# Fixed preparation steps beside each matrix product in an fp32 encoder layer

## The chip, the cores and the metric

One core of a Trainium2 chip runs the whole layer. The metric is the device time of one execution in microseconds (us); lower is better. The engines are PE (TensorE, the matrix products), ACT (ScalarE), DVE (VectorE), POOL (GpSimd) and SP (SyncE, which issues most DMAs). Each runs its own queue in order.

## The reference

For 512 tokens of width 1024, in fp32:

```
h = h + 1/2 * SwiGLU_1(RMSNorm(h))             # d_ff 2816: gate, up, down
u = RMSNorm(h) @ W_in
h = h + concat([MLA(u), DiffAttention(u)]) @ W_out
h = h + 1/2 * SwiGLU_2(RMSNorm(h))
h = h + sigmoid(RMSNorm(h) @ W_g + b_g) * RMSNorm(p @ W_p)
SwiGLU(u) = (silu(u @ w_gate) * (u @ w_up)) @ w_down
```

## The kernel before

**Precision.** A product of two fp32 matrices is three PE passes: each operand is split into a high part (a cast to fp32r, on ACT) and a low part (source minus high part, a DVE subtraction, `sub` at L97), and `mm3` adds high*high, high*low and low*high (L373 to L375). So every weight that streams in from HBM has to be cast and subtracted before PE can use it.

**The ffns.** Each takes its 22 blocks of 128 hidden columns in four groups (`FGROUPS`): one "plain" group of 4 and three of 6. A group computes gate and up for its blocks, and then the 8 row blocks of its down projection into `h`. The plain group multiplies straight away and meanwhile builds, from the normed activations, the operands that the other groups use (`Forms.build`: DVE, ACT and a little POOL work). The groups of 6 work in pairs of blocks: `pair` calls `seven` twice, once for gate and once for up. `seven` does a 2x2 block product in 7 block products instead of 8. Each product is 12 matmuls of 128x256 (4 contraction blocks x 3 passes). Three PSUM banks take them: `r2` products 1, 4 and 7, `r1` products 2 and 5, `r3` products 3 and 6. Between two products that share a bank, DVE or ACT must read what the first left there (L530, L531, L534, L537, L542, L545), and PE waits for that reading.

**Preparing weights.** `items` is the list of weight pieces in the order of use. A `Chunk` is one piece: load, cast, low part. A `Unit` serves one `seven`: it loads `ra`, `rb`, `rc` through SP; in `sums` POOL issues two DMAs that add further weights onto `rb` and `rc` in SBUF; then come casts and low parts for `xa`, `xb`, `xc`, two POOL additions in `ra` (L170, L171), and last cast and low part of `xs`, the halves of which are the left operands of products 1 (`S2`) and 6 (`S4`). Finished pieces lie in two pools of three tiles (`held` counts them); a unit takes three tiles, so a unit is prepared in one pool while the unit before it is used from the other.

**The written order.** In the ffns ACT, DVE and POOL run in the order in which the program is written. `advance()` writes the next step of the next item, or nothing if its pool is full, and subtracts the step's cost from `st["time"]`. `slot(us)` adds an allowance to `st["time"]`, capped at 1.5, and writes steps while it is positive. `nxt()` takes the next finished item, and writes its missing steps first if it is not finished; they are subtracted too. Between the ffns only PE's order is written by hand, and `chunk()`, which is `nxt(2)`, prepares some 26 chunks without any allowance.

**Around it.** `Norm` sums squares of `h` (square on ACT, addition on POOL at L319) and `col_rsqrt` multiplies that sum by ones on PE. `prep()` loads the latents' up-weights (`upraw`), `embed()` loads and splits `pT` and multiplies it, in turns of the attention loop that `FILL_STEPS` sets. `pe_norm()`, stepped beside the second ffn's down projections, reads its product back and sums squares. At the start, `first` holds the first gate and up chunks, loaded and split in halves.

Of the kernel before, what the change touches and what calls it, by code (L numbers as in the profile page):

```python
# [8 lines left out]
F32 = mybir.dt.float32  # L9
# [5 lines left out]
P = 128  # L15
S = 512
# [19 lines left out]

FILL_PRE = "TTTTTTTTTTTTTKTKTKTTT"
FILL_MID = "TKK"
FILL_STEPS = ("T", "TT", "TT", "TT", "T", "") + ("E", "") * 8
HEADS = "DDMDMDMMMMMM"  # L40

GC = {"ffn1": 0, "mix": 8, "ffn2": 16, "ple_in": 24, "ple_out": 32, "b_ple": 40,
# [7 lines left out]
def encoder_layer(ctx, tc, xT, pT, wst, gcols, rows, consts, out):  # L50
# [84 lines left out]
    class Unit:  # L135
        LO, HI = slice(0, S), slice(S, BLK)

        def __init__(self, which):
            self.which = which
            self.loads = [self.load_b, self.load_a]  # L140
            self.steps = [(0.0, self.sums, 0), (0.0, self.cast_a, 1), (1.2, self.cast_b, 1), (1.2, self.low_b, 0),
                          (0.0, self.cast_c, 0), (0.7, self.low_c, 0), (0.0, self.cast_s, 1), (1.2, self.low_s, 0)]

        def load_b(self):
            self.s0, self.s1 = take(BLK), take(BLK)
# [16 lines left out]
        def cast_b(self):  # L162
            self.xb = hl_tile(self.which, "xb")
            nc.scalar.copy(self.xb[:, 0, :], self.rb)
            sub(self.xa[:, 1, :], self.ra, self.xa[:, 0, :])

        def low_b(self):
# [10 lines left out]
        def low_c(self):  # L178
            sub(self.xc[:, 1, :], self.rc, self.xc[:, 0, :])

        def cast_s(self):
            self.xs = hl_tile(self.which, "xs")
            nc.scalar.copy(self.xs[:, 0, :], self.ra)  # L183

        def low_s(self):
            sub(self.xs[:, 1, :], self.ra, self.xs[:, 0, :])
            st["raws"] -= 1
            xa, xb, xc, xs = self.xa, self.xb, self.xc, self.xs

            self.out = [(xa, 0), (xa, S), (xb, 0), (xb, S), (xc, 0), (xs, 0), (xs, S)]  # L190
# [6 lines left out]
    def ffn_items():  # L197
        for f0, n, plain in FGROUPS:
            if plain:
                items.extend(Chunk(BLK) for _ in range(2 * n))  # L200
            else:
                items.extend(Unit(u % 2) for u in range(n))
            items.extend(Chunk(n * P, 0 if m < KT // 2 else 1) for m in range(KT))

    ffn_items()
    items.extend(Chunk(2 * 416) for _ in range(4))
# [29 lines left out]
        load_ahead()  # L236
        return True

    def slot(us, ahead=3):

        st["time"] = min(st["time"] + us, 1.5)
        load_ahead()
        while st["time"] > 0 and len(ready) < ahead and advance():
            pass

    def nxt(ahead=0):
        if used:
# [133 lines left out]
            mm3(ps, w[:, 0, c], w[:, 1, c], acts[k][:, 0, :], acts[k][:, 1, :], k == 0, k == n - 1)  # L381


    n1 = Norm("ffn1")
    pe_dram = drp.tile([KT, P, S], F32, name="pe_dram")
    rpe = const.tile([P, TT], F32, name="rpe")
    first = []
# [8 lines left out]
        nc.scalar.copy(it.hl[:, 0, a:b], it.raw[:, a:b])  # L396
        sub(it.hl[:, 1, a:b], it.raw[:, a:b], it.hl[:, 0, a:b])

    half = [(0, S), (S, BLK)]
    nc.scalar.dma_start(out=first[0].raw[:, :S], in_=first[0].src[:, :S])  # L400
    nc.scalar.activation(warm, warm, AF.Silu)
    nc.sync.dma_start(out=h[0], in_=xT[0])
    nc.sync.dma_start(out=first[1].raw[:, :S], in_=first[1].src[:, :S])
    for t in range(1, 4):
        nc.sync.dma_start(out=h[t], in_=xT[t])
    for it in first:
        nc.sync.dma_start(out=it.raw[:, S:], in_=it.src[:, S:])
    for t in range(4, KT):
        nc.sync.dma_start(out=h[t], in_=xT[t])
    st["raws"] = 2  # L410
    load_ahead()
    piece(first[0], 0, S)
    n1.add(0, False)
    piece(first[1], 0, S)
    for t in range(1, 4):
        n1.add(t, False)
    for it in first:
        piece(it, S, BLK)
    st["raws"] = 0
    for t in range(4, KT):  # L420
        n1.add(t, False)
    load_ahead()
    nc.sync.dma_start(out=cst, in_=consts)
    nc.sync.dma_start(out=row, in_=rows.partition_broadcast(P))
# [7 lines left out]
    for t in range(KT):  # L432
        n1.square(t)
        if t == 3:
            slot(3.0)
    held[0] -= 2

    def pe_norm():
        pe_acc = t2("pe_acc")
        for m in range(KT):  # L440
            pe = t2("pel")
            nc.gpsimd.dma_start(out=pe, in_=pe_dram[m])
            square_sum(pe_acc, pe, m == 0)
            yield
        r4 = col_rsqrt(pe_acc, DM)
        nc.vector.tensor_copy(out=rpe, in_=r4)
        yield
# [5 lines left out]
    class Forms:  # L453
# [10 lines left out]
        def build(self, kp):  # L464
            def v(t):
                return t.rearrange("p (a b) -> p a b", b=HS)

            def put(i, src):
                pg_ = page(f"fm{i}")
                d = pg_.rearrange("p x (a b) -> p x a b", b=HS)  # L470
                split(d[:, 0], d[:, 1], src)
                self.pg[kp][i] = pg_

            y = hl_tile(1, "y", F32)
            ks = (2 * kp, 2 * kp + 1, 2 * kp + 4, 2 * kp + 5)
            for i, k in enumerate(ks):
                nc.vector.scalar_tensor_tensor(out=y[:, i // 2, (i % 2) * S:(i % 2 + 1) * S], in0=h[k],
                                               scalar=g(self.name, k), in1=self.rbc, op0=ALU.mult, op1=ALU.mult)
                yield
            q = [y[:, i].rearrange("p (a b) -> p a b", b=S) for i in range(2)]  # L480
            b11, b12 = q[0][:, :, :HS], q[0][:, :, HS:]
            b21, b22 = q[1][:, :, :HS], q[1][:, :, HS:]
            n1, t2_, n3, n4 = [v(t2(f"f{i}")) for i in range(4)]
            nc.gpsimd.tensor_sub(n1, b11, b12)
            nc.gpsimd.tensor_sub(n3, b12, b22)
            for i, k in enumerate(ks):
# [11 lines left out]
            put(self.N4, n4)  # L498
            yield

        def at(self, i, k):
# [8 lines left out]
    MUL = 12 * 0.12  # L510

    def seven(forms, after=None):

        F_ = Forms
        A11, A12, S1, A22, S3, S2, S4 = nxt()
        r1, r2, r3 = psum("r1"), psum("r2"), psum("r3")
        q1, q2, q3 = t2("q1"), t2("q2"), t2("q3")
        lo, hi = slice(0, HS), slice(HS, S)

        def mul(r, left, i, start):  # L520
            x, c0 = left
            for k in range(4):
                c = slice(c0 + k * P, c0 + (k + 1) * P)
                bh, bl = forms.at(i, k)
                mm3(r[:, lo], x[:, 0, c], x[:, 1, c], bh, bl, start and k == 0, k == 3, skip_group_check=True)

        mul(r2, S2, F_.T2, True)
        slot(MUL)
        mul(r1, A11, F_.B11, True)
        nc.scalar.copy(q1[:, lo], r1[:, lo])  # L530
        nc.vector.tensor_sub(q1[:, hi], q1[:, lo], r2[:, lo])  # L531
        slot(MUL - 0.42)
        mul(r3, S1, F_.N1, True)
        nc.vector.tensor_add(q2[:, lo], r3[:, lo], q1[:, lo])  # L534
        slot(MUL - 0.42)
        mul(r2, S3, F_.N3, False)
        nc.vector.tensor_sub(q3[:, hi], r2[:, lo], q2[:, lo])  # L537
        slot(MUL - 0.42)
        mul(r1, A12, F_.B21, False)
        after(0, r1[:, lo])  # L540
        mul(r3, S4, F_.B22, False)
        nc.vector.tensor_add(q2[:, hi], r3[:, lo], q1[:, hi])  # L542
        after(1, q2[:, hi])
        mul(r2, A22, F_.N4, False)
        nc.vector.tensor_sub(q3[:, lo], r2[:, lo], q1[:, lo])  # L545
        after(2, q3)

    def ffn(norm, after, side=None, early=None):
        st_ = {}
# [16 lines left out]
        def pair(hts):  # L566
# [3 lines left out]
            def gate(i, c):  # L570
                if i < 2:
                    nc.scalar.activation(a0[:, i * HS:(i + 1) * HS], c, AF.Silu)
                    slot(MUL - 0.42 * i)
                else:
                    nc.scalar.activation(c, c, AF.Silu)
                    box["a1"] = c
                    slot(MUL - 0.42)

            def up(i, c):
                if i < 2:  # L580
                    nc.vector.tensor_mul(a0[:, i * HS:(i + 1) * HS], c, a0[:, i * HS:(i + 1) * HS])
                    slot(MUL - 0.42 * (i + 1))
                else:
                    nc.vector.tensor_mul(c, c, box["a1"])
                    put_ht(a0, hts)
                    put_ht(c, hts)
                    slot(MUL - 2.5)

            seven(forms, gate)
            seven(forms, up)  # L590
# [8 lines left out]
        for gi, (f0, n, plain) in enumerate(FGROUPS):  # L599
# [30 lines left out]
            for m in range(KT):  # L630
# [4 lines left out]
                last = gi == len(FGROUPS) - 1  # L635
                if last:
                    after(m)
                elif side is not None and gi > 0:
                    next(side, None)
                slot(0.68 * n - (1.5 if last else 0.75))  # L640
                build(2)

# [112 lines left out]
    def prep():  # L755

        up, off = [], 0
        for i, n in enumerate(UP):
            raw = raw_tile("upraw")
            nc.sync.dma_start(out=raw[:, :n], in_=wst[off:off + P * n].rearrange("(p c) -> p c", p=P))  # L760
            off += P * n
            uh, ul = page(f"uph{i}", (P, BLK), pool=scope["pgx"]), page(f"upl{i}", (P, BLK))
# [138 lines left out]
    def embed():  # L901
        pa = []
        for k in range(2):
# [2 lines left out]
            ah, al = t2("pTh", F32R), t2("pTl", F32R)  # L906
            split(ah, al, pt_)
            pa.append((ah, al))
        for m in range(KT):
            if m % 4 == 0:  # L910
                w = chunk()
# [415 lines left out]
```

## Time and profile before

| | |
|---|---|
| median of 3 runs | 1193.39 us (1191.41 to 1195.14) |
| the profiled execution | 1193.64 us |
| its span in the profile | 1191.9 us |
| PE busy | 1055.9 us, 89% of the span |
| DVE busy | 737.9 us, 62% |
| ACT busy | 505.4 us, 42% |
| POOL busy | 348.7 us, 29% |
| mean granted PE clock | 0.959 |

The span runs from the first to the last instruction; 1.7 us of the time lie outside it. PE's busy time counts overlapping matmuls and half-clock matmuls as busy, so the share says little about what stands between PE and its full speed: the waits do, stage by stage. The first ffn runs from 0 to about 410 us, projections and attention to about 692, the second ffn to about 1140, and the gate of the embedding to the end.

### The profile page before, as it was taken

Reading aid. Unit: us, or ns where it says so; the run is one execution under the profiler, and the core shown is the slowest. Engines: PE = TensorE matmul, PEld = TensorE weight load, DVE = VectorE, ACT = ScalarE, POOL = GpSimd, SP = SyncE. Lnnn points to the kernel's source line nnn. Section 1 sums busy time; section 2 is a strip of 40 time slices with the busy share of each in tenths; the row PEclk is TensorE's granted clock in tenths of the full one; section 3 lists DMA queues with packets and bytes.
Section 4 is the critical chain, followed back from the end, with each engine's and each line's share of the span. In section 5 each row is a group of like instructions: output and inputs, shape, how many; then the busy total and the mean of one; then the engine's idle time right before and its main releaser. Section 6 shows DMA issues by size and latency. Waiting matters only on the chain.

```text
span 1191.9 us, 15846 instructions
## 1 busy us (share of the span) xinstructions
PE 1055.9 (89%) x6076; PEld 912.4 (77%) x6076; DVE 737.9 (62%) x1230; ACT 505.4 (42%) x824; POOL 348.7 (29%) x305
## 2 busy tenths in 40 slices
PE   8987898889889999979999995777897789888998
PEld 6867887888888887856678873557885788788887
DVE  5686755663665658886888626455653574466574
ACT  6343422342333546575786423223432342234341
POOL 4224402430431300054543121014324440243130
PEclk9999999999999998989999997788999899999999
DMA  6156535644562542221120210145535653564251
GB/s 240 27 148 154 127 117 135 155 115 138 148 145 79 164 131 87 75 85 53 54 72 18 89 53 27 45 123 144 136 104 165 157 123 113 139 150 107 97 195 53
DMA packets 50667, 133.73 MB, mean 112 GB/s; under 512 B 5952, under 2 KB 6336, under 8 KB 50592
## 3 DMA queue, kind: packets, MB, share of 16 engines
q1 hardware_dynamic: 36720, 104.78, 26.9%
q0 software_dynamic: 12432, 25.57, 11.9%
q10 hardware_dynamic: 1440, 2.39, 0.5%
q8 instruction: 47, 0.77, 0.3%
q14 instruction: 28, 0.23, 0.1%
HBM read 126.02 MB, written 6.29 MB: 111 GB/s over the span
## 4 chain that ended last, share of the span: by engine, by line
PE 52%; DVE 13%; POOL 11%; ACT 10%; DMA 7%; issue 7%; SPq 0%; ACTq 0%; POOLq 0%; DVEq 0%
POOL ra L170 5%; PE ps_d L375 5%; PE ps_d L374 5%; PE ps_d L373 5%; PE r L373 4%; POOL ra L171 4%; PE r L375 3%; PE r L374 3%; DVE xa L97 3%; ACT xa L160 3%; ACT xs L183 2%; DMA ra<-in_wst_dram 2%; PE ps_in L373 2%; PE ps_in L374 2%; PE ps_in L375 2%
## 5 line engine op out<-in xcount | busy, mean ns | idle before, releaser
L124 ACT CAST hl<-raw 128x768 fp32r<-128x768 f32 (+3 forms) x112 | 97.4, 887 | 131.1 <-PE ps_d L375 43.4
L97 DVE TENSOR_TENSOR hl<-raw,hl 128x768 fp32r<-128x768 f32 (+3 forms) x116 | 129.8, 1131 | 36.9 <-ACT hl L124 34.4
L375 PE MATMUL ps_d<-ht,hl 128*128 128x512 f32 x352 | 141.0, 401 | 10.8 <-DVE hl L97 10.8
L373 PE MATMUL ps_d<-ht,hl 128*128 128x512 f32 x352 | 141.0, 400 | 7.0 <-ACT hl L124 3.8
L374 PE MATMUL ps_d<-ht,hl 128*128 128x512 f32 x352 | 140.8, 400 | 0.2 <-DVE ht L94 0.2
L170 POOL TENSOR_TENSOR ra<-ra,rb 128x512 f32<-128x512 f32 x36 | 72.7, 2019 | 231.6 <-DVE xa L97 228.6
L373 PE MATMUL r<-fm,xb 128*128 128x256 f32 x288 | 84.3, 293 | 16.9 <-DVE q L537 16.9
L375 PEld LDWEIGHTS ps_d<-ht,hl 128*128 128x128 f32 x352 | 68.2, 194 | 28.9 <-DVE hl L97 14.7
L183 ACT CAST xs<-ra 128x1024 fp32r<-128x1024 f32 x36 | 37.7, 1047 | 115.5 <-POOL ra L171 115.5
L373 PEld LDWEIGHTS ps_d<-ht,hl 128*128 128x128 f32 x352 | 67.9, 193 | 21.6 <-ACT hl L124 4.2
L97 DVE TENSOR_TENSOR xs<-ra,xs 128x1024 fp32r<-128x1024 f32 x36 | 44.3, 1230 | 63.0 <-ACT xs L183 63.0
L373 PE MATMUL r<-sa,xa 128*128 128x256 f32 x288 | 82.5, 287 | 0.0
L374 PE MATMUL r<-sa,xa 128*128 128x256 f32 x288 | 82.3, 286 | 0.0
L375 PE MATMUL r<-sa,xa 128*128 128x256 f32 x288 | 82.1, 285 | 0.0
L374 PE MATMUL r<-fm,xb 128*128 128x256 f32 x288 | 81.4, 283 | 0.0
L375 PE MATMUL r<-fm,xb 128*128 128x256 f32 x288 | 81.3, 282 | 0.0
L374 PEld LDWEIGHTS ps_d<-ht,hl 128*128 128x128 f32 x352 | 68.3, 194 | 14.8 <-DVE ht L94 0.5
L319 POOL TENSOR_TENSOR acc<-acc,sq 128x512 f32<-128x512 f32 x28 | 39.2, 1401 | 131.8 <-ACT sq L318 131.5
L97 DVE TENSOR_TENSOR xa<-ra,xa 128x1024 fp32r<-128x1024 f32 x36 | 44.1, 1224 | 47.4 <-ACT xa L160 47.4
L373 PE MATMUL r<-fm,xc 128*128 128x256 f32 x144 | 44.7, 311 | 31.9 <-DVE q L531 31.9
L373 PEld LDWEIGHTS r<-fm,xb 128*128 128x128 f32 x288 | 54.9, 191 | 22.6 <-DVE q L537 22.6
L155 POOL DMA_DIRECT2D rb<-in_wst_dram x36 | 31.9, 886 | 100.7 <-DMA rb<-in_wst_dram 50.0
(333 smaller groups left out, 3091.3 us busy)
## 6 DMA issues: line engine op xcount, KB each, us to landing
raw<-in_wst_dram SPq DMA_DIRECT2D x44, 512.0 KB, 3.4
rb<-in_wst_dram SPq DMA_DIRECT2D x36, 512.0 KB, 5.2
ra<-in_wst_dram SPq DMA_DIRECT2D x36, 512.0 KB, 3.6
raw<-in_wst_dram SPq DMA_DIRECT2D x48, 384.0 KB, 3.6
rc<-in_wst_dram SPq DMA_DIRECT2D x36, 256.0 KB, 5.2
rb<-in_wst_dram POOLq DMA_DIRECT2D x36, 256.0 KB, 4.3
rc<-in_wst_dram POOLq DMA_DIRECT2D x36, 256.0 KB, 6.9
raw<-in_wst_dram SPq DMA_DIRECT2D x19, 256.0 KB, 2.6
```

The lines of the kernel that those rows point to most:

```text
L97: nc.vector.tensor_sub(dst_l, src, dst_h.bitcast(F32))
L124: nc.scalar.copy(self.hl[:, 0, :self.n], self.raw[:, :self.n])
L155: nc.gpsimd.dma_start(out=self.rb[:, self.LO], in_=self.s1[:, self.HI], accum_op=ALU.add)
L160: nc.scalar.copy(self.xa[:, 0, :], self.ra)
L170: nc.gpsimd.tensor_add(ra[:, LO], ra[:, LO], self.rb[:, LO])
L171: nc.gpsimd.tensor_add(ra[:, HI], ra[:, HI], ra[:, LO])
L183: nc.scalar.copy(self.xs[:, 0, :], self.ra)
L319: (eng or nc.gpsimd).tensor_add(acc, acc, sq)
L373: MM(ps, lhsT=wh, rhs=ah, start=start, stop=False, **kw)
L374: MM(ps, lhsT=wh, rhs=al, start=False, stop=False, **kw)
L375: MM(ps, lhsT=wl, rhs=ah, start=False, stop=stop, **kw)
```

## The change

- **Units.** Eight steps become eleven: the low part of `xa` is a step of its own, and cast and low part of `xs` are done in two halves, the half for product 1 first. Units use the pools in the opposite turn, and the plain group's down chunks all use pool 0.
- **Fixed steps.** In `seven`, `steps(n)` writes 1, 2, 2, 1, 1, 2, 2 steps behind products 1 to 7 (11 in all). The slots in `gate` and `up` go.
- **Slots elsewhere.** `slot(us)` sets the allowance afresh, without a cap or a limit on finished items.
- **First bank.** ACT copies `r2` behind product 1 into `q2[:, hi]`; the DVE subtraction that read `r2` there now reads that copy, and stands behind product 4.
- **Start.** The first two chunks come in pieces of 256, 256 and 512 columns instead of two halves, in another order of DMAs; the first norm's additions are on DVE; one load less is counted ahead.
- **Side work.** `pe_norm` loads through SP, two ahead, and takes two steps behind each down block of the second group instead of one in the second and third; `upraw` has pages of its own; `embed` loads and splits `pT` in a turn of its own, five attention steps earlier; the pool tile of `Forms.build` is counted.

```diff
-FILL_STEPS = ("T", "TT", "TT", "TT", "T", "") + ("E", "") * 8
+FILL_STEPS = ("T", "TTE", "TT", "TT", "T", "") + ("E", "") * 8
...
-            self.steps = [(0.0, self.sums, 0), (0.0, self.cast_a, 1), (1.2, self.cast_b, 1), (1.2, self.low_b, 0),
-                          (0.0, self.cast_c, 0), (0.7, self.low_c, 0), (0.0, self.cast_s, 1), (1.2, self.low_s, 0)]
+            self.steps = [(0.0, self.sums, 0), (0.1, self.cast_a, 1), (0.1, self.cast_b, 1), (1.2, self.low_a, 0),
+                          (1.2, self.low_b, 0), (0.1, self.cast_c, 0), (0.7, self.low_c, 0),
+                          (0.1, self.cast_s0, 1), (0.7, self.low_s0, 0), (0.1, self.cast_s1, 0),
+                          (0.7, self.low_s1, 0)]
...
+        def low_a(self):
             sub(self.xa[:, 1, :], self.ra, self.xa[:, 0, :])
...
-        def cast_s(self):
+        def cast_s0(self):
             self.xs = hl_tile(self.which, "xs")
-            nc.scalar.copy(self.xs[:, 0, :], self.ra)
+            nc.scalar.copy(self.xs[:, 0, self.LO], self.ra[:, self.LO])
+
+        def low_s0(self):
+            sub(self.xs[:, 1, self.LO], self.ra[:, self.LO], self.xs[:, 0, self.LO])
...
-                items.extend(Unit(u % 2) for u in range(n))
-            items.extend(Chunk(n * P, 0 if m < KT // 2 else 1) for m in range(KT))
+                items.extend(Unit(1 - u % 2) for u in range(n))
+            items.extend(Chunk(n * P, 1 if m < KT // 2 and not plain else 0) for m in range(KT))
...
-    def slot(us, ahead=3):
+    def slot(us):
 
-        st["time"] = min(st["time"] + us, 1.5)
+        st["time"] = us
         load_ahead()
-        while st["time"] > 0 and len(ready) < ahead and advance():
+        while st["time"] > 0 and advance():
             pass
+
+    def steps(n):
+        load_ahead()
+        for _ in range(n):
+            advance()
...
-    n1 = Norm("ffn1")
+    n1 = Norm("ffn1", nc.vector)
...
+    for it in first:
+        load_piece(it, 0, 256, nc.scalar)
     nc.scalar.activation(warm, warm, AF.Silu)
+    for a, b in ((256, 512), (512, BLK)):
+        t0 = a // 128 - 2
+        for t in (t0, t0 + 1):
+            nc.sync.dma_start(out=h[t], in_=xT[t])
+        for it in first:
+            load_piece(it, a, b)
...
-        for m in range(KT):
-            pe = t2("pel")
-            nc.gpsimd.dma_start(out=pe, in_=pe_dram[m])
-            square_sum(pe_acc, pe, m == 0)
+        pes = []
+        for m in range(KT + 2):
+            if m < KT:
+                pes.append(t2("pel"))
+                nc.sync.dma_start(out=pes[m], in_=pe_dram[m])
+            if m >= 2:
+                square_sum(pe_acc, pes[m - 2], m == 2)
...
         mul(r2, S2, F_.T2, True)
-        slot(MUL)
+        nc.scalar.copy(q2[:, hi], r2[:, lo])
+        steps(1)
         mul(r1, A11, F_.B11, True)
         nc.scalar.copy(q1[:, lo], r1[:, lo])
-        nc.vector.tensor_sub(q1[:, hi], q1[:, lo], r2[:, lo])
-        slot(MUL - 0.42)
+        steps(2)
         mul(r3, S1, F_.N1, True)
         nc.vector.tensor_add(q2[:, lo], r3[:, lo], q1[:, lo])
-        slot(MUL - 0.42)
+        steps(2)
         mul(r2, S3, F_.N3, False)
         nc.vector.tensor_sub(q3[:, hi], r2[:, lo], q2[:, lo])
-        slot(MUL - 0.42)
+        nc.vector.tensor_sub(q1[:, hi], q1[:, lo], q2[:, hi])
+        steps(1)
         mul(r1, A12, F_.B21, False)
         after(0, r1[:, lo])
+        steps(1)
         mul(r3, S4, F_.B22, False)
         nc.vector.tensor_add(q2[:, hi], r3[:, lo], q1[:, hi])
         after(1, q2[:, hi])
+        steps(2)
         mul(r2, A22, F_.N4, False)
         nc.vector.tensor_sub(q3[:, lo], r2[:, lo], q1[:, lo])
         after(2, q3)
+        steps(2)
...
-                elif side is not None and gi > 0:
-                    next(side, None)
+                elif side is not None and gi == 1:
+                    for _ in range(2):
+                        next(side, None)
...
-            raw = raw_tile("upraw")
+            raw = page("upraw", (P, BLK), F32)
...
             pa.append((ah, al))
+        yield
         for m in range(KT):
```

## Rows read from the trace of the kernel before

**Rows 1.** Waits of PE: who waited for whom, us in total, times, longest.
```profile
PE r L373 <- DVE q L531: 31.9, 30, 2.8
PE r L373 <- ACT xs L183: 19.3, 3, 11.6
PE r L373 <- DVE q L537: 16.9, 28, 0.6
PE ps_g L373 <- ACT hl L124: 13.1, 2, 8.4
...
PE r L375 <- DVE xs L97: 9.1, 6, 1.8
PE ps_pe L373 <- ACT pTh L93: 7.5, 1, 7.5
...
PE ps_q L373 <- ACT latT L732: 3.3, 1, 3.3
...
PE ps_g L373 <- ACT act_ffn L361: 2.2, 1, 2.2
PE ps_ss L329 <- POOL acc L319: 2.1, 1, 2.1
```
**Rows 2.** PE in order of time: start, duration, idle time before it.
```profile
1051.16 0.28 PE L373 MATMUL r<-sa,xa 128*128 128x256 f32 x1
...
1053.92 0.28 PE L375 MATMUL r<-fm,xb 128*128 128x256 f32 x1
1054.73 0.39 PE L373 MATMUL r<-fm,xc 128*128 128x256 f32 x1 [0.53 <-DVE q L531]
```
**Rows 3.** DVE in order of time, in an up `seven` and at 91 us.
```profile
1051.98 1.23 DVE L97 TENSOR_TENSOR xa<-ra,xa 128x1024 fp32r<-128x1024 f32 x1 [1.64 <-ACT xa L160]
...
1054.26 0.41 DVE L531 TENSOR_TENSOR q<-q,r 128x256 f32<-128x256 f32 x1
1054.59 1.44 DVE L97 TENSOR_TENSOR xc<-rc,xc 128x512 fp32r<-128x512 f32 x1
...
1058.29 1.22 DVE L97 TENSOR_TENSOR xs<-ra,xs 128x1024 fp32r<-128x1024 f32 x1 [1.93 <-ACT xs L183]
...
91.31 0.68 DVE L97 TENSOR_TENSOR xc<-rc,xc 128x512 fp32r<-128x512 f32 x1
```
**Rows 4.** Stretches: length, busy us (instructions) of PE, PEld, DVE, ACT, POOL; PE clock.
```profile
1053.92:1078.08 24.16, 21.17 (x171) 20.36 (x169) 16.14 (x24) 10.03 (x15) 11.05 (x9) 1.00 0.58 143
...
39.00:93.80 54.80, 45.88 (x193) 36.33 (x191) 47.63 (x66) 25.06 (x39) 14.46 (x10) 0.96 0.34 93
715.80:809.40 93.60, 59.25 (x195) 43.90 (x195) 51.82 (x68) 27.25 (x42) 14.11 (x10) 0.78 0.23 66
...
24.30:39.00 14.70, 12.63 (x48) 10.14 (x47) 1.70 (x3) 1.64 (x3) 6.24 (x8) 0.77 0.21 71
445.80:455.30 9.50, 5.88 (x18) 4.76 (x17) 4.78 (x7) 5.18 (x9) 0.00 (x0) 0.64 0.46 157
527.20:540.60 13.40, 5.13 (x18) 3.27 (x16) 9.79 (x22) 7.30 (x18) 7.14 (x7) 0.62 0.24 79
```
**Rows 5.** POOL in order of time: the first addition of a unit, twice.
```profile
87.34 1.29 POOL L170 TENSOR_TENSOR ra<-ra,rb 128x512 f32<-128x512 f32 x1 [5.26 <-DVE xa L97]
...
1053.29 2.18 POOL L170 TENSOR_TENSOR ra<-ra,rb 128x512 f32<-128x512 f32 x1 [6.58 <-DVE xa L97]
```
**Rows 6.** Groups of ACT by line: busy us, mean ns, idle before.
```profile
L160 ACT CAST xa<-ra 128x1024 fp32r<-128x1024 f32 x36 | 37.5, 1041 | 37.9 <-DMA ra<-in_wst_dram 30.9 <-PE r L375 7.1
...
L176 ACT CAST xc<-rc 128x512 fp32r<-128x512 f32 x36 | 22.3, 620 | 5.4 <-DMA rc<-in_wst_dram 5.4
...
L530 ACT COPY q<-r 128x256 f32<-128x256 f32 x36 | 13.2, 366 | 1.9 <-PE r L375 1.9
```
**Rows 7.** DMA issues of POOL: count, KB each, median us from issue to landing.
```profile
rb<-in_wst_dram POOLq DMA_DIRECT2D x36, 256.0 KB, 4.3
rc<-in_wst_dram POOLq DMA_DIRECT2D x36, 256.0 KB, 6.9
```

More of the change, by code (lines that the diff above doesn't have):

```diff
@@ L179, in low_c, with cast_s1, low_s1 @@
             sub(self.xc[:, 1, :], self.rc, self.xc[:, 0, :])
-        def cast_s(self):
+        def cast_s0(self):
             self.xs = hl_tile(self.which, "xs")
-            nc.scalar.copy(self.xs[:, 0, :], self.ra)
-        def low_s(self):
-            sub(self.xs[:, 1, :], self.ra, self.xs[:, 0, :])
+            nc.scalar.copy(self.xs[:, 0, self.LO], self.ra[:, self.LO])
+        def low_s0(self):
+            sub(self.xs[:, 1, self.LO], self.ra[:, self.LO], self.xs[:, 0, self.LO])
+        def cast_s1(self):
+            nc.scalar.copy(self.xs[:, 0, self.HI], self.ra[:, self.HI])
+        def low_s1(self):
+            sub(self.xs[:, 1, self.HI], self.ra[:, self.HI], self.xs[:, 0, self.HI])
             st["raws"] -= 1
@@ L397, in piece, with load_piece @@
         sub(it.hl[:, 1, a:b], it.raw[:, a:b], it.hl[:, 0, a:b])
-    half = [(0, S), (S, BLK)]
-    nc.scalar.dma_start(out=first[0].raw[:, :S], in_=first[0].src[:, :S])
+    def load_piece(it, a, b, eng=nc.sync):
+        eng.dma_start(out=it.raw[:, a:b], in_=it.src[:, a:b])
+    for it in first:
+        load_piece(it, 0, 256, nc.scalar)
     nc.scalar.activation(warm, warm, AF.Silu)
[L402 to L407, printed above, removed]
+    for a, b in ((256, 512), (512, BLK)):
[4 more added lines that the diff above has]
+            load_piece(it, a, b)
     for t in range(4, KT):
@@ L411, in encoder_layer @@
     load_ahead()
[L412 to L421, printed above, removed]
+    for a, b in ((0, 256), (256, 512), (512, BLK)):
+        piece(first[0], a, b)
+        n1.add(a // 128, False)
+        piece(first[1], a, b)
+        for t in range(a // 128 + 1, b // 128):
+            n1.add(t, False)
+    st["raws"] -= 2
     load_ahead()
@@ L434, in encoder_layer @@
         if t == 3:
-            slot(3.0)
+            steps(2)
     held[0] -= 2
@@ L472, in put @@
                 self.pg[kp][i] = pg_
+            held[1] += 1
             y = hl_tile(1, "y", F32)
@@ L498, in build @@
             put(self.N4, n4)
+            held[1] -= 1
             yield
@@ L508, in at @@
             return pg_[:, 0, c], pg_[:, 1, c]
-    MUL = 12 * 0.12
     def seven(forms, after=None):
@@ L546, in seven @@
         after(2, q3)
+        steps(2)
     def ffn(norm, after, side=None, early=None):
@@ L572, in gate @@
                     nc.scalar.activation(a0[:, i * HS:(i + 1) * HS], c, AF.Silu)
-                    slot(MUL - 0.42 * i)
                 else:
@@ L576, in gate @@
                     box["a1"] = c
-                    slot(MUL - 0.42)
             def up(i, c):
@@ L581, in up @@
                     nc.vector.tensor_mul(a0[:, i * HS:(i + 1) * HS], c, a0[:, i * HS:(i + 1) * HS])
-                    slot(MUL - 0.42 * (i + 1))
                 else:
@@ L586, in up @@
                     put_ht(c, hts)
-                    slot(MUL - 2.5)
             seven(forms, gate)
```

## The prediction

> **What bounds the kernel now.** I read the waits of PE first, then PE in order of time inside one `seven`, then DVE beside it, then stretches. PE is the engine that sets the end; the question is what it waits for.
>
> Between 1051.16 and 1053.92 us PE starts 23 matmuls of 256 columns, 0.120 us each [rows 2]. A product of 12 is then 1.44 us, a `seven` of 84 is 10.08 us, a pair 20.16 us. A pair takes 24.16 us, at full clock [rows 4]: 4.0 us, a sixth, is waiting. Nearly all of it has two names: product 4 waits for L531, which reads `r2`, and product 7 for L537, which reads it again [rows 1]. The DVE queue says why [rows 3]: L531 starts at 54.26, though `r1` was there earlier, because the low parts of `xa` and `xb` were written before it. L537 likewise stands behind the low part of `xs`, for which DVE idles 1.93 us until the cast comes, and that cast needs POOL's two additions. So PE pays for preparation that is written in front of its own reads.
>
> The second loss is the second ffn's plain group. The same work, from the broadcast of the norm to the first `seven`, takes 54.8 us in the first ffn and 93.6 in the second, with 193 and 195 matmuls, and the granted clock there averages 0.78 [rows 4]. PE waits 13.1 us there for two casts of `hl` [rows 1]. The code gives the cause: each chunk between the ffns lowers `st["time"]` by about 1.3 without an allowance, some 30 in all, and the capped slots cannot pay that back within the group; every chunk is then prepared by `nxt()` at the last moment, behind the evacuations in ACT's queue.
>
> The rest is single waits: 11.6 us once for `xs` (the start of the second ffn's third group), 7.5 for `pTh`, 3.3 for `latT`, 2.2 and 2.1 in the first 30 us, 9.1 in six for the low part of `xs` [rows 1]. Several are followed by half clock [rows 4].
>
> **The change, part by part.**
>
> *`seven`.* Product 4 now waits only for ACT's copy of `r2`, 0.37 us [rows 6], written behind product 1, two products earlier: gone, with 2.5 us of cover; if ACT is later than that, its lateness comes back as the wait. To see what is late next I count steps. A unit has 11 and a `seven` writes 11, so the phase stays; after a group's first pair the `sums` of the next unit fall behind product 7, `cast_a` behind product 1, `cast_b` and `low_a` behind 2, `low_b` (with POOL's additions) and `cast_c` behind 3, `low_c` behind 4, `cast_s0` behind 5, `low_s0` behind 6, `low_s1` behind 7. For an up `seven` with product 1 at 0 and no waits, with the durations of [rows 3, 5, 6]:
>
> ACT: copy of `r2` 1.44 to 1.8, `cast_a` to 2.85, copy of `r1` to 3.25, `cast_b` to 4.3, `cast_c` behind it. DVE: `low_a` 2.9 to 4.1, L534's sum at 4.4 to 4.8, then `low_b`. POOL's first addition begins at 4.1 and holds `low_b` until 5.4, since each of the two is longer when they meet: 2.18 against 1.29 us, 1.44 against 0.68 [rows 3, 5]. `low_b` to 6.6, second addition to 7.9, `q3` at 7.0, the moved subtraction (now two SBUF operands, so it waits too) to 8.3, `low_c` to 9.0, then three reads of 0.41 to 10.2, `low_s0` to 10.9. Product 7, due at 8.64, needs `q3` of 7.0: its wait is gone. Product 1 of the next `seven` needs the low part of `xs` at its third matmul, 10.08 + 0.24 = 10.32: a wait of up to 0.6. In a gate `seven` two of the three reads fall to ACT, which ends DVE at 10.1: none. I take 0.3 as the mean. DVE has 16.14 us of work per 24.16 us pair [rows 4], which would be 80% of 20.2: not the bound.
>
> The DMAs of `sums`: POOL issues them when its additions end at 7.9. `rb` lands 4.3 later, at 12.2 or 2.1 of the next `seven`, before `cast_b` at 3.25. `rc` is issued 0.6 later and lands after 6.9 [rows 7], at 5.3; `cast_c` ends at 5.9, and `low_c` comes at 8.3. Both are hidden, `rc` with 2.4 us to spare.
>
> The sum: 31.9 + 16.9 = 48.8 us idle in 58 waits [rows 1]. Each costs more: between the starts 53.92 and 54.73 there are 0.81 us where 0.12 would do, 0.69 lost for 0.53 shown [rows 2]. With 0.16 for each, 58. Thirty `sevens` at 0.3 give 9 back: **-49**. Bounds: -58 with no wait, -29 if half stays.
>
> *Second ffn's plain group.* `slot` no longer carries the debt, so chunks are written as in the first ffn. 93.6 - 54.8 = **-39**; bounds -30 and -42 (some DVE work before `pe_norm` and `Forms` is as crowded as in the first ffn, which keeps its waits).
>
> *Group starts.* The unit behind the down projection of a group of 6 is written during its blocks 5 to 7, 4 us each, and is ready before product 1. Three of the six waits for the low part of `xs` go: about **-5**. The 11.6 us wait stood behind POOL, which alternated `pe_norm`'s loads, additions and the unit's `sums`. Now SP loads, but the `col_rsqrt` of `pe_norm` falls behind down block 5, and its `pow` stands in POOL's queue ahead of `sums`: block 5's end + 3 us + 6.9 for `rc` + cast and low part, against two blocks of 4.1 us until product 1: some 3.5 us stay. **-9**, with the clock. The starts behind the plain groups keep most of their wait (the chain of loads, `sums` and casts is the same, on a DVE busy for 47.6 of 54.8 us [rows 4]): **-2**. Half clock after these waits, into the first `seven`: **-6**, as an estimate of four stretches of about 3 us at half speed.
>
> *Start.* The norm's additions on DVE, which has little to do there (1.70 of 14.7 us), end the wait of 2.1, and with it the half clock after it: (1 - 0.77) x 14.7 = 3.4 [rows 1, 4]. Smaller pieces land sooner; of the 2.2 us wait I take 1. **-6.5**.
>
> *Middle.* `upraw` no longer waits for the three raw tiles: 3.3 and half of 5.9 busy us at half clock, of which I take **-5**. `pT`'s loads are off PE's path: 7.5 and half of 5.13: **-9.5**, since the split then lies steps before its use. Outside the ffns ACT and DVE are not ordered by hand, so both could be lost (0 each).
>
> *At nothing.* The pools' opposite turn is a mirror image. Two casts and low parts of 512 for one of 1024 cost 0.2 us more on engines with room. One load less counted ahead changes little, since a load waits for its tile either way. The counted tile of `Forms` holds back the first unit's `xs` until `Forms` ends, two down blocks before its use; without that cover it would be part of the wait at the starts behind the plain groups.
>
> The sum is 49 + 39 + 5 + 9 + 2 + 6 + 6.5 + 5 + 9.5 = 131. Against the profiled execution's 1193.64 (0.25 over the median) that gives 1062.6, and against the median 1062.
>
> **A rule against it.** A subtraction and a POOL addition that meet take turns [rows 3, 5]. The Trainium skill, "SBUF — State Buffer", section "Who interferes with whom", says that a DVE instruction with two SBUF inputs contends with a POOL instruction that reads SBUF, the later one waiting for all of the earlier; the trace agrees (1.44 for 0.68 us). By that rule the moved subtraction, which read PSUM before, can also lose a whole addition; I have one such wait in the layout, a second would add up to 1.3 us to each `seven`.
>
> **The rivals.** *DVE and POOL in turns* (chance 0.2): each `seven` keeps one more turn at product 1, about 0.8 us in 30 `sevens`: 1062 + 24 = 1086. For it: `low_s0` ends within 0.6 us of its need. Against: gate `sevens` have room. The rule named above speaks for this case. *The phase slips* (0.08): if a unit runs one step later, `sums` behind product 1, then `low_a` and `low_b` both follow product 3, `low_s0` ends near 12.5, and a `seven` takes about the 12.1 of now: +49, 1111. Against: the pools never refuse one of the 11 steps in the steady state as I count it. *The plain group stays slow* (0.07): if the casts are late for the evacuations themselves and not for the debt, +39, 1101; the first ffn, with the same evacuations, speaks against it. *Slower* (0.04): at 10.4 us per unit the DMAs carry 1.16 times the bytes per time. If `rc` lands late enough that every `seven` waits, the gain is gone when 36 wait 131/36 = 3.6 us more than I have; with 2.4 us to spare that needs a landing of 6.9 + 2.4 + 3.6, about 13 us from issue, nearly twice the median. *The forecast* has 0.61, with a range of its own of 1043 to 1078.
>
> **How the numbers follow.** Low end: no wait at product 1 (-9), nothing at the group starts (-5), the plain group at -42, some of the middle: 1040. High end: the first rival and the plain group's rival, 1101, with part of the middle lost; the phase rival is mostly left out. So 1040 to 1105. Faster by over 0.3% (what this measurement can tell): the first four cases, 0.95; within it 0.01; slower 0.04.
>
> **What would show it.** L531 gone from PE's waits at product 4, nothing at product 7; a pair of 20.2 to 20.8 us; the stretch from the broadcast to the first `seven` near 55 us in both ffns; no `pTh` and `acc` waits. Wrong would be a wait of PE for the low part of `xs` in each `seven` over 1 us, casts of `rc` ending idle time of ACT beyond 3 us, or casts still written behind the evacuations.

## The result and the profile after

The changed kernel takes 1082.16 us (median of 4 runs, 1079.43 to 1084.05) beside 1192.4 for the kernel before on the same chip: ratio 0.9072, 95% interval 0.9045 to 0.9098, 110 us less. The forecast was 1062 in 1040 to 1105, so the sign and the range held and the middle was 20 us too low. The span fell from 1191.9 to 1077.7 us.

Each stage does the same work in both kernels, so its length can be set side by side. (One thing moves: the last product of `pe_norm`, 0.95 us, goes from the last of the "other three stretches" into the row above them.) The edges are the starts of the same PE instructions in the two timelines, which are of one profiled execution each; the first ffn's last down blocks, 32.8 us in both, are left out. The forecast's terms stand in the last column.

| stage | before, us | after, us | difference | forecast |
|---|---|---|---|---|
| start to the first broadcast | 37.75 | 29.69 | -8.1 | -6.5 |
| first ffn: broadcast to first `seven` | 53.68 | 53.70 | 0.0 | -2 |
| the six blocks of six `sevens`, both ffns | 444.2 | 394.2 | -50.0 | -60 (49 + 5 + 6) |
| second ffn: down blocks ahead of the third group's sevens | 44.47 | 34.98 | -9.5 | -9 |
| the other three stretches of down blocks ahead of a group of 6 | 98.96 | 98.01 | -0.9 | 0 |
| first projection to the first product of the second ffn | 280.1 | 269.5 | -10.6 | -14.5 |
| second ffn: first product to first `seven` | 116.15 | 76.58 | -39.6 | -39 |
| last down blocks and the end | 83.8 | 88.3 | +4.5 | 0 |

The page of the changed kernel, busy time by engine (share, instructions) and PE's granted clock in 40 slices:

```profile
span 1077.7 us, 16017 instructions
...
PE 1030.5 (96%) x6076; PEld 902.8 (84%) x6076; DVE 752.4 (70%) x1275; ACT 525.7 (49%) x898; POOL 329.7 (31%) x290
...
PEclk9998999999999999999999999989999999999999
```

Stretches of the changed kernel, the columns as in [rows 4]: the two plain stretches, one steady pair, and the matmuls behind a wait at 188 us.

```profile
29.69:83.39 53.70, 46.32 (x198) 37.21 (x196) 45.12 (x64) 25.30 (x41) 13.26 (x9) 0.95 0.31 90
670.13:724.00 53.87, 46.53 (x198) 37.31 (x196) 44.47 (x63) 25.39 (x41) 12.35 (x9) 0.96 0.31 88
969.00:989.43 20.43, 20.41 (x170) 20.21 (x169) 15.75 (x25) 9.93 (x18) 3.45 (x2) 1.00 0.53 142
188.20:190.80 2.60, 2.60 (x12) 2.60 (x13) 1.99 (x4) 1.22 (x3) 1.24 (x2) 0.50 0.83 228
```

The steady pair takes 20.43 us, inside the 20.2 to 20.8 that were to be seen (it is the last of its group; the pair before it takes as long), and the two plain stretches are now alike. The next view, the waits of PE in the changed kernel (us in total, times, longest), answers to [rows 1].

```profile
PE r L388 <- ACT q L546: 13.2, 4, 3.6
PE r L388 <- ACT xs L187: 9.1, 3, 4.0
PE ps_d L388 <- ACT ht L93: 6.4, 2, 3.2
PE ps_bc L338 <- POOL r L316: 2.8, 1, 2.8
PE r L390 <- DVE xs L97: 2.6, 3, 1.7
PE ps_ds L1059 <- DVE pe L937: 2.0, 1, 2.0
```

The 48.8 us before products 4 and 7 are gone, and so are `hl`, `pTh`, `latT` and `acc`. The first line is new: product 4 waits for L546, the very copy of `r2` by ACT that the change put in, four times at the start of a group behind a group of 6. PE in order of time at the first of them:

```profile
184.46 0.28 PE L390 MATMUL r<-fm,xb 128*128 128x256 f32 x1
188.16 0.58 PE L388 MATMUL r<-fm,xc 128*128 128x256 f32 x1 [3.42 <-ACT q L546]
188.54 0.41 PE L389 MATMUL r<-fm,xc 128*128 128x256 f32 x1
```

And ACT's queue at that place:

```profile
180.66 1.05 ACT L162 CAST xa<-ra 128x1024 fp32r<-128x1024 f32 x1 [1.01 <-DMA ra<-in_wst_dram]
184.27 1.04 ACT L166 CAST xb<-rb 128x1024 fp32r<-128x1024 f32 x1 [2.56 <-DMA rb<-in_wst_dram]
187.22 0.62 ACT L180 CAST xc<-rc 128x512 fp32r<-128x512 f32 x1 [1.91 <-DMA rc<-in_wst_dram]
187.75 0.36 ACT L546 COPY q<-r 128x256 f32<-128x256 f32 x1
```

The three casts belong to the unit behind the one in use. `slot` no longer caps its allowance at 1.5; by the code a down block now has 3.33 us to write, so a whole unit is finished early and the last down block writes the casts of the next, ahead of the `seven`. (The old limit of three finished items would not have stopped it: only one is finished there.) The first cast waits for its load, the other two for the adding DMAs, and the copy, whose bank was full soon after product 1 (181.7), stands behind them until 187.75. The twelve matmuls that follow go at a granted clock of 0.50, that is at 1.2 GHz: 2.6 us where 1.44 would do, on top of the 3.4 us of waiting.

### The profile page after: what moved, and what is told of

Its sections match the earlier page's. It is cut to its first block, busy times and chain, and to the rows that moved or that the text cites. A ratio compares the mean times of both kernels' runs of the same rounds, so it can differ in the third digit from the quotient of the medians.

```text
span 1077.7 us, 16017 instructions
## 1 busy us (share of the span) xinstructions
PE 1030.5 (96%) x6076; PEld 902.8 (84%) x6076; DVE 752.4 (70%) x1275; ACT 525.7 (49%) x898; POOL 329.7 (31%) x290
## 4 chain that ended last, share of the span: by engine, by line
PE 75%; DVE 8%; DMA 6%; ACT 5%; issue 4%; POOL 2%; POOLq 0%; SPq 0%; ACTq 0%; DVEq 0%
PE r L390 11%; PE r L388 11%; PE r L389 11%; PE ps_d L389 5%; PE ps_d L390 5%; PE ps_d L388 4%; DMA rc<-in_wst_dram 4%; PE ps_in L388 3%; PE ps_in L389 3%; PE ps_in L390 3%; DVE hl L97 2%; PE ps_pt L1116 1%; PE ps_wo L388 1%; PE ps_wo L390 1%; PE ps_wo L389 1%
## 5 line engine op out<-in xcount | busy, mean ns | idle before, releaser
L97 DVE TENSOR_TENSOR hl<-raw,hl 128x768 fp32r<-128x768 f32 (+4 forms) x118 | 125.0, 1069 | 50.1 <-ACT hl L124 48.9
L388 PE MATMUL ps_d<-ht,hl 128*128 128x512 f32 x352 | 138.5, 393 | 6.4 <-ACT ht L93 6.4
L389 PE MATMUL ps_d<-ht,hl 128*128 128x512 f32 x352 | 138.6, 394 | 0.5 <-DVE ht L94 0.5
L390 PE MATMUL ps_d<-ht,hl 128*128 128x512 f32 x352 | 138.4, 393 | 0.0
L174 POOL TENSOR_TENSOR ra<-ra,rb 128x512 f32<-128x512 f32 x36 | 50.0, 1389 | 201.7 <-DVE xa L97 183.1
L388 PEld LDWEIGHTS ps_d<-ht,hl 128*128 128x128 f32 x352 | 66.8, 190 | 21.0 <-ACT ht L93 7.2
L389 PEld LDWEIGHTS ps_d<-ht,hl 128*128 128x128 f32 x352 | 66.9, 190 | 14.8 <-DVE ht L94 1.1
L390 PEld LDWEIGHTS ps_d<-ht,hl 128*128 128x128 f32 x352 | 66.8, 190 | 14.6 <-DVE hl L97 0.8
L175 POOL TENSOR_TENSOR ra<-ra 128x512 f32<-128x512 f32 x36 | 74.2, 2060 | 2.8
L97 DVE TENSOR_TENSOR xb<-rb,xb 128x1024 fp32r<-128x1024 f32 x36 | 58.7, 1630 | 12.8 <-ACT xb L166 12.8
L334 POOL TENSOR_TENSOR acc<-acc,sq 128x512 f32<-128x512 f32 x21 | 29.3, 1395 | 110.5 <-ACT sq L333 110.5
L388 PEld LDWEIGHTS r<-sa,xa 128*128 128x128 f32 x288 | 57.3, 199 | 0.0
L389 PEld LDWEIGHTS r<-sa,xa 128*128 128x128 f32 x288 | 57.2, 199 | 0.0
```

Of the source, the lines that this page charges most:

```text
L97: nc.vector.tensor_sub(dst_l, src, dst_h.bitcast(F32))
L174: nc.gpsimd.tensor_add(ra[:, LO], ra[:, LO], self.rb[:, LO])
L175: nc.gpsimd.tensor_add(ra[:, HI], ra[:, HI], ra[:, LO])
L334: (eng or nc.gpsimd).tensor_add(acc, acc, sq)
L388: MM(ps, lhsT=wh, rhs=ah, start=start, stop=False, **kw)
L389: MM(ps, lhsT=wh, rhs=al, start=False, stop=False, **kw)
```

## The experiments

**e1: the bank read by DVE again.**

```diff
         mul(r2, S2, F_.T2, True)
-        nc.scalar.copy(q2[:, hi], r2[:, lo])
         steps(1)
         mul(r1, A11, F_.B11, True)
         nc.scalar.copy(q1[:, lo], r1[:, lo])
+        nc.vector.tensor_sub(q1[:, hi], q1[:, lo], r2[:, lo])
         steps(2)
...
-        nc.vector.tensor_sub(q1[:, hi], q1[:, lo], q2[:, hi])
```

> The changed kernel with the reading of r2 done as before: no copy by ACT, DVE's subtraction from the bank written behind product 2. Theory of the fixed order (what freed product 4 is that no low part is written between product 1 and that reading): PE waits for it 0 to 0.3 us in a steady seven, 1080 to 1090 us. Rival, the copy by ACT is what freed product 4: the wait for the reading comes back at about 1 us (0.53 to 1.06 in the kernel before) in 30 sevens, 1100 us or more. The waits of 3.4 us at the starts behind groups of 6 stay by both, since the copy of r1 stands behind the same casts.

1099.69 us, ratio 0.9222 (0.9186 to 0.9258): in time next to the rival's 1100, but not by its wait. The waits of PE:

```profile
PE r L388 <- DVE q L549: 17.6, 5, 4.5
PE r L390 <- DVE xs L97: 10.2, 15, 2.3
```

In the steady `sevens` product 4 waits for nothing, with DVE's reading just as before: the fixed order (with its eleven smaller steps) freed it, not the copy. The 17 us come from elsewhere: of the four long waits behind groups of 6, three grow (3.4, 3.4 and 3.6 us become 4.1 to 4.5), against the expectation; a fifth, of 1.7, is new; and the low part of `xs` is late by 0.56 in 12 `sevens`.

**e2: the debt forgiven, in the kernel before.**

```diff
     n3 = Norm("ple_in")
+    st["time"] = 0.0
     ffn(n2, n3.add, pe_norm())
```

> The kernel before with one line more: st[time] is set to 0 ahead of the second ffn. Theory of the debt: the stretch from the broadcast of the norm to the first seven falls from 93.6 to about 55 us, so 1192 - 39 = 1153 us, and the sevens keep their waits (31.9 and 16.9 us). Rival, the casts are late for the evacuations themselves: no change over 5 us, 1187 or more.

1155.59 us, ratio 0.9688 (0.9655 to 0.9721): 38.6 us from one line. The stretch from the broadcast to the first `seven`, which had 93.6 us [rows 4] (92.4 between the edges used here):

```profile
714.95:767.89 52.94, 45.25 (x198) 36.07 (x196) 44.44 (x63) 25.55 (x40) 13.17 (x10) 1.00 0.32 95
```

The debt was the whole cause of the slow plain group, and the gain adds to that of the `sevens`, whose waits stay here (27.5 us for L531).

**e3: the copy alone, in the kernel before.**

```diff
         mul(r2, S2, F_.T2, True)
+        nc.scalar.copy(q2[:, hi], r2[:, lo])
         slot(MUL)
...
-        nc.vector.tensor_sub(q1[:, hi], q1[:, lo], r2[:, lo])
...
         nc.vector.tensor_sub(q3[:, hi], r2[:, lo], q2[:, lo])
+        nc.vector.tensor_sub(q1[:, hi], q1[:, lo], q2[:, hi])
```

> The kernel before with the copy of r2 by ACT behind product 1 and the subtraction from that copy behind product 4, nothing else. If the copy is what frees product 4: the wait of 31.9 us in 30 goes and what it costs, 0.16 more each, so 1192 - 37 = 1155 us. If the written order of the low parts is what counts: DVE's next readings (r3 before product 6, r2 again before product 7) stand as late as before, the waits move there, and less than 12 us is won: 1180 us or more.

1228.11 us, ratio 1.0311 (1.0265 to 1.0358): 34 us slower, beyond the rival. The wait for L531 (31.9 us) is gone and the one before product 7 has grown from 16.9 to more than both:

```profile
PE r L373 <- DVE q L537: 48.4, 28, 1.8
```

DVE in order of time in one `seven`:

```profile
1084.53 1.23 DVE L97 TENSOR_TENSOR xs<-ra,xs 128x1024 fp32r<-128x1024 f32 x1 [1.92 <-ACT xs L183]
1085.67 0.42 DVE L537 TENSOR_TENSOR q<-r,q 128x256 f32<-128x256 f32 x1
```

L537 stands behind the low part of `xs`, and that behind the same casts and additions as before; PE merely reaches the same queue earlier. In the pair of [rows 4] the kernel before waits four times, 0.53 and 0.60 us in one `seven`, 1.25 and 0.60 in the other, all at a clock of 1.00. Here PE waits for L537 once in each `seven`, about 1.78 us, and in this pair the clock is 0.51 (1.2 GHz) behind both waits:

```profile
1073.30:1076.60 3.30, 3.30 (x18) 3.30 (x17) 0.42 (x1) 0.80 (x2) 0.00 (x0) 0.51 0.90 275
1072.22:1100.15 27.93, 24.15 (x168) 23.33 (x168) 16.92 (x24) 10.78 (x17) 11.05 (x8) 0.88 0.52 132
```

The pair takes 27.93 us instead of 24.16: 0.7 us more of waiting (there is also one of 0.16), and the rest is half clock (18 matmuls in 3.3 us where 2.16 would do, and the ends of that stretch, twice in a pair). Not every pair is like this one: of the 26 waits of about 1.78 us in e3, 15 have half clock behind them (0.66 granted over the 5 us from the wait's end) and 11 have none (1.00). The six blocks of `sevens` together are 27.8 us longer than before, most of the loss.

**e4: only the sums written ahead.** While a finished unit waits, the slots write the DMAs of the next one and stop before its casts.

```diff
-        while st["time"] > 0 and advance():
+        while st["time"] > 0 and not (any(isinstance(r, Unit) for r in ready) and isinstance(items[-1], Unit)
+                                      and len(items[-1].steps) < 11) and advance():
             pass
```

> The changed kernel; while a finished unit waits for its seven, the slots of the down projection write only the DMAs of the unit behind it, not its casts. Theory (ACT's copy of r2 in the first seven of a group stands behind casts of the second unit that wait for their DMAs): the waits of PE for that copy (13.2 us in 4) go, and the half clock behind them (about 1 us each), so 1082 - 13 to 17 = 1065 to 1069 us; the pairs inside a group stay at 20.2 to 20.8 us. Rival, the first seven of a group is late for its own operands or banks: the wait comes back under another name at the same place, 1077 us or more. Second rival: the second unit itself is late then, a wait for xb, xc or xs of over 2 us before the second seven, 1075 to 1090 us.

1063.01 us, ratio 0.8913 (0.888 to 0.8946): 19 us less than the changed kernel. The copy (L547 in this kernel) is in no wait any more. ACT at the same group start, and the six `sevens` of that group in one stretch (the changed kernel takes 66.03 us for them, from 180.27 to 246.30):

```profile
182.78 0.37 ACT L547 COPY q<-r 128x256 f32<-128x256 f32 x1 [2.26 <-PE r L391]
183.04 1.05 ACT L162 CAST xa<-ra 128x1024 fp32r<-128x1024 f32 x1
184.22 0.37 ACT L550 COPY q<-r 128x256 f32<-128x256 f32 x1
185.21 1.05 ACT L166 CAST xb<-rb 128x1024 fp32r<-128x1024 f32 x1 [0.62 <-DMA rb<-in_wst_dram]
```

```profile
181.14:242.16 61.02, 60.99 (x505) 60.58 (x504) 47.80 (x71) 31.49 (x54) 24.55 (x19) 1.00 0.66 166
```

61.02 us beside 60.48 for 504 matmuls at 0.120: here the written casts were the whole of it, and neither banks nor operands are late in the first `seven`. So it is in two more of the four starts behind groups of 6; at the second ffn's third group, waits of 0.3 to 1.1 us for `xs` stay.

**e11: both, the sums ahead and the bank read by DVE** (the edits of e4 and e1 together).

> The kernel with only the sums written ahead (e4) with r2 read by DVE behind product 2 as in e1. In e1's trace the four long waits got 1.1 us longer each and 12 pairs had one wait of 0.56 us for the low part of xs that the changed kernel does not have. If the copy of r2 by ACT is worth those 12 (0.72 us each in PE's starts), they stay without the long ones: 1063 + 9 = 1071 to 1075 us. Rival, they were an after-effect of the long waits: under 4 of them, 1061 to 1067 us.

1072.2 us, ratio 0.8987 (0.8958 to 0.9017): 9 us behind e4, with the 12 waits of 0.56 us still there. DVE shows how the copy earns them:

```profile
951.49 0.42 DVE L550 TENSOR_TENSOR q<-q,r 128x256 f32<-128x256 f32 x1 [2.31 <-ACT q L549]
951.83 1.22 DVE L97 TENSOR_TENSOR xa<-ra,xa 128x1024 fp32r<-128x1024 f32 x1
```

The subtraction waits 2.31 us for ACT, and the low part of `xa`, whose cast had ended at 950.4, waits behind it; POOL's additions and the low part of `xs` follow later by as much. So the copy is worth 9 us, but through what stands behind the reading, not through product 4.

**e5: three small parts undone.**

```diff
-    n1 = Norm("ffn1", nc.vector)
+    n1 = Norm("ffn1")
...
-            raw = page("upraw", (P, BLK), F32)
+            raw = raw_tile("upraw")
...
-FILL_STEPS = ("T", "TTE", "TT", "TT", "T", "") + ("E", "") * 8
+FILL_STEPS = ("T", "TT", "TT", "TT", "T", "") + ("E", "") * 8
...
             pa.append((ah, al))
-        yield
```

> The changed kernel with three small parts undone, each in a stretch of its own: the first norm's additions back on POOL, the latents' up-weights back in the three raw tiles, and the split of pT back in the turn in which it is used (with the turn plan of before). By the forecast's terms: the wait for acc of 2.1 us and its half clock come back in the first 31 us (+4 to +5.5), the wait for latT of 3.3 and half clock (+5), the wait for pTh of 7.5 and half clock (+9.5): 1082 + 19 = 1101 us. Rival, the pieces and the order of loads at the start do the start's work alone (first 31 us within 1 us), and the middle gives back only the 11 us by which its stretch got shorter: 1093 us.

1096.25 us, ratio 0.9205 (0.9174 to 0.9237), between the two. Its waits:

```profile
PE ps_pe L388 <- ACT pTh L93: 7.5, 1, 7.5
...
PE ps_ss L344 <- POOL acc L334: 5.8, 1, 5.8
```

The stretch to the first broadcast is 37.55 us, as long as before: the additions on DVE are worth 7.9 us, and all that the smaller pieces won would have turned into a longer wait for `acc` (5.8 us instead of 2.1). In the middle `pTh` is back with its 7.5 us, but the stretch from the first ffn's last down blocks to the second ffn is only 4.9 us longer, because the 2.0 us wait for `pe` in the attention, which the earlier split brought, goes, with some small ones. The wait for `latT` does not return, so the pages of `upraw` are not what ended it. In the kernel before, SP issued the last of the three up-weight loads 3.3 us after the first `lat` matmul (443.94 against 440.66), in e5 2.0 us ahead of it (415.78 against 417.81); which of the other edits brought that was not run.

**e6 and e9: `xs` whole.** The edit of e6 put the whole low part into the last of the four steps, not into that of the first half as its expectation says; e9 has it in the second of the four.

```diff
-            nc.scalar.copy(self.xs[:, 0, self.LO], self.ra[:, self.LO])
+            nc.scalar.copy(self.xs[:, 0, :], self.ra)
...
         def low_s0(self):        # e9; in e6 this line stands in low_s1
-            sub(self.xs[:, 1, self.LO], self.ra[:, self.LO], self.xs[:, 0, self.LO])
+            sub(self.xs[:, 1, :], self.ra, self.xs[:, 0, :])
```

> The changed kernel with cast and low part of xs each done whole in the step of the first half (the steps of the second half stay, empty). If DVE's layout is as tight as the forecast drew it (low part of the first half at 10.9 against a need at 10.3), the whole low part ends 0.55 us later and nearly each seven waits for it: some 30 waits of 0.5 to 0.9 us, 1097 to 1110 us. Rival, DVE has room in a seven: under 8 such waits, within 4 us of 1082. The starts behind plain groups get up to 1 us longer by both.

> The changed kernel with cast and low part of xs each done whole, both in the steps of the first half, two steps ahead of where e6 wrote the low part. If the place in the written order is what cost e6 its 78 us (its low part stood behind the readings of product 7), nearly all of it comes back: waits for xs of at most 0.3 to 0.8 us in some sevens, 1082 to 1095 us. Rival, the size of the piece is what costs (a whole low part cannot end ahead of product 1): waits of over 1 us in most sevens, 1115 us or more.

e6: 1160.26 us, ratio 0.9738 (0.9697 to 0.978). e9: 1093.28, ratio 0.9167 (0.9126 to 0.9209). The wait for the low part of `xs`, first in e6:

```profile
PE r L390 <- DVE xs L97: 64.6, 30, 3.5
```

and in e9:

```profile
PE r L389 <- DVE xs L97: 12.6, 18, 1.5
```

Same instructions, two steps apart: 67 us. In e6 the low part stands behind the reading of product 7 (and behind the two low parts of `ht` in an up `seven`), so the first product of the next `seven` cannot but wait. The size of the piece costs 11 us (e9): there are 12 new waits of 0.55 us. Most of the net loss, 8.5 us, lies in the two blocks of `sevens` behind plain groups; in the other four the new waits are nearly made up for by shorter ones for the copy of `r2` (6.7 us in the four starts, 13.2 in the changed kernel).

**e8 and e10: the rest of the new waits.** On top of e4: the last step of `pe_norm` moved into the third group's down blocks, and each scaling of `pe2` written where it is used.

```diff
-                elif side is not None and gi == 1:
+                elif side is not None and (gi == 2 or gi == 1 and m < 5):
...
-    for m in range(KT):
-        nc.vector.scalar_tensor_tensor(out=pe2[m], in0=pe2[m], scalar=g("ple_out", m), in1=pe_bc,
-                                       op0=ALU.mult, op1=ALU.mult)
...
+        if c.start in (0, None):
+            nc.vector.scalar_tensor_tensor(out=pe2[m], in0=pe2[m], scalar=g("ple_out", m), in1=pe_bc,
+                                           op0=ALU.mult, op1=ALU.mult)
         a = t2("ga")
```

> The kernel with only the sums written ahead, with two more edits. The last step of pe_norm (col_rsqrt, whose power stood on POOL ahead of the sums of the third group of the second ffn) moves into the down blocks of that third group, and the scalings of pe2 are written where each block needs them, not ahead of the last norm's v. Expected: the wait for the last broadcast (4.4 us, and half clock of 3.4 us behind it, 1.7 lost) goes, the wait of 1.1 + 0.6 us at the third group's start goes: 1063 - 6 - 2 = 1055 us. Rival, the broadcast waits for the norm's sums themselves: it stays over 3 us, 1061 us.

1055.24 us, ratio 0.885 (0.8824 to 0.8876): the best version by what was understood, 27 us under the changed kernel. The wait for the last broadcast is gone, and the down blocks ahead of the second ffn's third group take 32.67 us (34.98 in the changed kernel). e10 adds a fourth raw tile:

```diff
-RAWS = 3
+RAWS = 4
...
-    pgp = ctx.enter_context(tc.tile_pool(name="pgp", bufs=27))
+    pgp = ctx.enter_context(tc.tile_pool(name="pgp", bufs=26))
```

> The version of e8 with a fourth raw tile (and one page less in the page pool). If the first unit behind a plain group is late because its loads wait for a free raw tile, each load comes one chunk's time (2.7 us) earlier, the two waits for xs of 4.2 us shrink to 1.5 to 2 us with part of their half clock, and the time falls by 5 to 8 us, to 1047 to 1050. Rival, the chain of sums, casts and additions behind the loads or DVE's queue sets it: no change over 2 us, 1053 to 1057.

1054.27 us, ratio 0.8825 (0.88 to 0.8851), no different from e8. Waits at the starts of the sevens, first in e8:

```profile
PE r L389 <- ACT xs L187: 8.4, 2, 4.2
...
PE r L391 <- DVE xs L97: 2.7, 3, 1.4
```

and in e10:

```profile
PE r L391 <- DVE xs L97: 4.8, 2, 2.7
PE r L389 <- ACT xs L187: 3.5, 2, 2.0
```

The casts came earlier, as the first theory said (8.4 to 3.5 us), and DVE's low part took over a part of the wait (2.7 to 4.8). The time is what the rival said. Both theories were half right, and behind these starts both limits stand close together.

## Why the prediction was right, and where it was off

**The `sevens`: right in size, and only half right in cause.** The steps that I counted come in the order in which I counted them, and a steady pair takes 20.43 us. The forecast had 0.3 us per `seven` left for the low part of `xs`; the trace has 0.18 in a pair (the third matmul at 969.42, not at 969.24). But I put product 4 down to ACT's copy. e1 shows that the copy is not needed for it: with the fixed order alone product 4 is free. e3 shows that the copy alone frees product 4 too, but hands the wait to product 7, and the kernel is 34 us slower.

**Group starts: the step that failed.** I wrote "if ACT is later than that, its lateness comes back as the wait", and that a unit behind a group of 6 "is written during its blocks 5 to 7" and is ready. I then drew ACT's queue for a steady `seven` only. At a group's start the uncapped slot writes also the casts of the unit behind it, ahead of the copy, and these wait for DMAs. One of them, at 930.2 us, followed 3.1 us in which ACT stood idle for `rc`; idle time of over 3 us before such a cast was one of my signs of being wrong. That cost 19 us in the four starts (1082.16 against 1063.01 in e4; in three of the groups the six `sevens` take 5.0 to 5.2 us longer than in e4, in one, where the wait was 2.8 us and the clock stayed at 1.00, 3.7). Without it the blocks of `sevens` take 375.7 us, 68.5 under the kernel before, where the forecast had 60. So the -50 that came out is two misses that partly cancel: 18.5 us lost at the starts, 8.5 more won than forecast elsewhere.

**The plain group: right**, -39.6 for -39, and e2 shows the debt alone to be the cause. **The third group's start: right**, -9.5 for -9. Of the 2.3 us more that e8 wins there, with `pe_norm`'s last step out of the way, 0.95 is that step's product and comes back in the next down blocks (33.62 for 32.67); the rest speaks for the power ahead of `sums` that I had named. **Starts behind plain groups: off by 2**, nothing was won.

**The start: right in size** (-8.1 for -6.5), mis-sized in its parts. I gave the additions on DVE 5.5 and the pieces 1; e5 shows that without the additions nothing is won at all.

**The middle: one term too large, one right for the wrong reason.** -10.6 for -14.5. The earlier split of `pT` was to give 9.5 and gave 4.9 in e5, since it brought a wait for `pe` with it. That leaves 5.7 beside the 5 for `latT`, whose wait went; but e5 has this gain without the pages of `upraw`, so the cause that I named is not it, and the true one stays open.

**The end: not in the forecast.** +4.5 us. DVE in order of time before the last broadcast:

```profile
1032.46 2.86 DVE L1209 SCALAR_TENSOR_TENSOR pe<-pe,gc,pe_bc 128x512 f32<-128x512 f32 x4 [1.46 <-DMA pe<-pe_dram]
1035.23 0.15 DVE L347 TENSOR_SCALAR v<-ps_ss 128x4 f32<-128x4 f32 x1
```

The norm's `v`, 0.15 us of work, stands behind all eight scalings; of the last four, shown here, the first waited for a DMA. In the kernel before it stood behind two:

```profile
1147.00 1.40 DVE L1189 SCALAR_TENSOR_TENSOR pe<-pe,gc,pe_bc 128x512 f32<-128x512 f32 x2
1148.33 0.15 DVE L332 TENSOR_SCALAR v<-ps_ss 128x4 f32<-128x4 f32 x1
```

The program text is the same in both at this place, and DVE's order is not written by hand there; why it fell differently was not looked into. I had not looked at what is written outside the ffns. e8, which writes each scaling later, has no such wait.

**At nothing.** The pools' opposite turn, the load less counted ahead and the counted tile of `Forms` were not run by themselves.

**The rival of DVE and POOL in turns** gave 1086, nearer to 1082 than the forecast, but not by its mechanism. The turns are there. DVE and POOL in order of time in a steady gate `seven`:

```profile
974.20 1.83 DVE L97 TENSOR_TENSOR xb<-rb,xb 128x1024 fp32r<-128x1024 f32 x1
975.03 2.15 POOL L175 TENSOR_TENSOR ra<-ra 128x512 f32<-128x512 f32 x1
...
976.29 1.18 DVE L556 TENSOR_TENSOR q<-q,q 128x256 f32<-128x256 f32 x1
```

The moved subtraction takes 1.18 us here and 0.41 at 191.47 us, where POOL ran no addition. The Trainium skill, "SBUF — State Buffer", section "Who interferes with whom", says that a DVE instruction with two SBUF inputs contends with a POOL instruction that reads SBUF; the trace agrees. But in this pair it delays no product: the readings behind it still come in time, and three of e4's six blocks of `sevens` run within 1% of PE's full speed. The debt and the phase rivals are out (53.87 us; no slip), and no landing came near 13 us (the latest of `rc` from POOL: 8.4).

## What to carry to other kernels

In an engine's in-order queue a read that frees a bank is as late as the slowest instruction written in front of it. So fix the place of preparation beside each product, and put nothing that waits for a DMA ahead of such a read: issue the DMA early, and write the cast behind. An allowance that is set freely can write too much as well as too little. Draw the queue for the first round of a loop too, not only for the steady one; and when one wait is taken away, look for the next instruction that the consumer will meet in the same queue, since a freed product that runs into it can lose more than it won (e3).

## What the runs showed of the hardware

- Nearly the same idle time, cut differently, cost far more: 2.98 us in four waits of at most 1.25 left a pair at a granted clock of 1.00 (2.4 GHz) [rows 4]; in e3, of 26 waits of about 1.78 us, 15 had some 3.3 us near 0.51 (1.2 GHz) behind them and 11 had none. What decides between the two is not shown. The kernel of e3 is 34 us slower with PE waiting 48.4 us for DVE's readings, beside 48.8 before [rows 1].
- With the same bytes moved in a span shorter by a tenth, the adding DMAs of POOL landed about as before: medians of 4.7 and 6.4 us for `rb` and `rc`, beside 4.3 and 6.9 [rows 7].
